# Chunk rows of a state-space scan taken in twos, on one Trainium2 core

## The chip, the cores and the metric

The kernel runs on one core of a Trainium2 chip. The metric is device time in microseconds (us) from the start to the end of one execution; the median of several runs is compared. Engines are named as in the profile: PE is the matrix engine (TensorE), PEld its weight load, DVE is VectorE, ACT is ScalarE, POOL is GpSimd, SP is the engine whose queue issues most of the DMAs.

## What is computed

One layer of a decoder with two branches: a causal pooling branch and a Mamba-2 (SSD) branch, over a prompt of 1024 positions and 8 short samples, merged by gates. The change touches only the prompt's SSD scan. In the reference it is this (cut to the loop body):

```python
def step(h, inp):                    # one chunk of Q = 128 positions
    xq, dq, Bq, Cq = inp
    acs = jnp.cumsum(dq * Ag, axis=1)
    ...
    decay = jnp.exp(jnp.where(mask, seg, -jnp.inf))
    cb = jnp.einsum('bign,bjgn->bijg', Cq, Bq)
    att = cb[..., None] * decay * dq[:, None]
    y = jnp.einsum('bijge,bjgep->bigep', att, xq)
    y = y + jnp.einsum('bign,bige,bgepn->bigep', Cq, jnp.exp(acs), h)
    last = acs[:, -1]
    w_in = jnp.exp(last[:, None] - acs) * dq
    h = h * jnp.exp(last)[..., None, None] + jnp.einsum('bjgn,bjge,bjgep->bgepn', Bq, w_in, xq)
    return h, y
```

There are 4 groups of 8 heads of 64 channels, a state of 128 and 8 chunks, so 32 steps, here called rows. Afterwards y + D*x is multiplied by silu(z), normalized, and multiplied by the rows of `w_ssm_out`.

## The kernel before

The work runs in three stages. First come the projections (up to some 765 us of the span). Then comes the chunk stage, some 765 to 1055 us, which the change concerns. Last comes a tail with the last output products.

**A row.** `chunk(g, c)` is a Python generator; each `next` on it traces one step of a row's instructions:

- load: DMAs on SP's queue for `dec` (the cumulated decays, broadcast to all partitions), `bc` (B and C) and `xb` (x)
- exponentials: `cE` by one ACT instruction (L1510), a triangular select on POOL (`far`, L1240), eight ACT exponentials of 128 columns (`exps`, L1244)
- middle: PE transposes x into the PSUM tile `px` (L1517), transposes B and multiplies B by C into `pbc` (L1519, L1520); ACT copies `bt` and C (L1522, L1524); DVE makes `xd` and `xw` (L1528, L1530) and multiplies `dec` and `cE` by PSUM columns (L1535, L1537)
- sums: PE's matmul `pu` of `bt` and `xw` with 512 columns (L1542, the state's increment), then `inner` (L1256, L1259): for each head one product of `xd` with `dec` and, from the second chunk on, one of the state with `cE`. Each has 64 weight columns, and two heads at a time write the upper and the lower half of the PSUM partitions. POOL and DVE make the new state `hn` (L1548, L1550), and DVE adds D*x into the sums (L1554)
- finish: DVE, ACT and POOL multiply by silu(z), split the result into two parts for the later product and sum its squares (`finish`, L1470 to L1481)

**Pieces.** Between these steps PE works on "pieces": `pieces()` yields after each block of 12 matmuls with 384 or 352 columns (`gemm_`, L221) into one of the three PSUM banks of `PA`. These are the products of the pooling branch and of earlier groups. `RATE = 2.56` pieces go with one row. DVE or ACT evacuates each.

**What sets the order.** In the chunk stage the instructions of PE and of SP's queue keep the order in which they are traced (`in_line(order)`, with `ORDER = ("PE","SP")`). Those of ACT, DVE and POOL are ordered by the planner, by its own estimate of times and with the traced order as priority; `tc.high_priority()` moves instructions forward in that priority. A tile's buffer is given to the next tile of the same tag when the last instruction that uses it, anywhere in the program, is done.

**The loop** (L1850 to L1871) takes one row at a time. In PE's order it gives: middle of row i+1, about one piece, `pu` and `inner` of row i, one or two pieces. PSUM: `PB` has four banks (`px`, `pbc`, and the sums `pi`), `PC` a single one (`pu`). From the ninth row on, one step of `wos` (the split of the output weights `w_o`, L1772 to L1825) goes with each row.

**The tail** starts with four more pieces and the sum of squares over partitions (L1903, L1904), from which ACT makes `rstd` (L1905, L1907). Later GpSimd adds rows of `x_prompt` in 16 accumulating DMAs (`plus_x`, L2065), the only DMAs that GpSimd issues.

## Time and profile before

| | us |
|---|---|
| runs | 1219.95, 1220.73, 1222.36; median 1220.73 |
| profiled execution, span from first to last instruction | 1219.3 |
| PE busy | 1203.2 (99% of the span) |
| DVE busy | 937.9 (77%) |
| POOL busy | 758.1 (62%) |
| ACT busy | 654.7 (54%) |
| chunk stage cut at 776.7 to 1053.5 | 276.8: PE 274.4, DVE 225.5, POOL 180.8, ACT 171.9 |

The profiled execution has no time of its own beside the span. The span is 1.4 us below the median of the runs, which is what lies around it; the granted clock is 0.998. In the rows of a timeline the columns are: start, length, engine, line, operation, tiles written and read, shapes, count of merged instructions, and in brackets the engine's idle time before it and what ended it. The lengths of matmuls overlap, since they are pipelined; the starts are what one subtracts. A PE instruction in float32 stands as two passes.

### The profile page before, as it was taken

To read this page: it belongs to the slowest core of one execution; us is meant where nothing else is said; L and a number is where in the kernel's file an instruction comes from. 1 tells how busy PE (TensorE), PEld (TensorE's weight loads), DVE (VectorE), ACT (ScalarE), POOL (GpSimd) and SP (SyncE) were. 2 spreads that over 40 slices of the span, in tenths; PEclk is the share of its full clock that TensorE was granted. 3 is DMA by queue.
4 is the path that set the end of the run, shared out by engine and by line. 5 is a ranking of instruction groups with operands and counts; after the bars stand their busy time and mean duration, and the time that the engine had idled before them with its cause. 6 is when DMAs were issued, how large, how long until landed. Compare 5 with 4: busy or idle time off the path is not lost.

```text
span 1219.3 us, 25493 instructions
## 1 busy us (share of the span) xinstructions
PE 1203.2 (99%) x9330; PEld 1127.1 (92%) x9330; DVE 937.9 (77%) x1587; ACT 654.7 (54%) x1491; POOL 758.1 (62%) x677
## 2 busy tenths in 40 slices
PE   9999999999999999999999999999999999999997
PEld 8879999999999999999989899989888898999885
DVE  6993788877989578876676664686877889679976
ACT  6854366565656656454544344566676656312435
POOL 1137868875978778664676766155677758422661
PEclk9999999999999999999999999999999999999999
DMA  9835455564565545443656566898779888585794
GB/s 347 307 136 212 134 155 179 157 232 151 165 188 181 171 149 187 137 143 122 205 187 210 172 198 215 317 314 265 264 257 293 270 279 279 186 313 174 233 213 150
DMA packets 169845, 257.48 MB, mean 211 GB/s; under 512 B 32048, under 2 KB 88120, under 8 KB 169720
## 3 DMA queue, kind: packets, MB, share of 16 engines
q1 hardware_dynamic: 89256, 163.38, 40.3%
q10 hardware_dynamic: 78160, 88.27, 21.4%
q0 software_dynamic: 2304, 4.20, 2.0%
q8 instruction: 74, 1.21, 0.4%
q14 instruction: 51, 0.42, 0.1%
HBM read 170.69 MB, written 85.10 MB: 210 GB/s over the span
## 4 chain that ended last, share of the span: by engine, by line
PE 84%; DVE 6%; DMA 5%; ACT 3%; issue 1%; POOL 1%; SPq 0%; ACTq 0%; DVEq 0%
PE mm L410 23%; PE ps L410 23%; PE mm L221 14%; PE pc L410 5%; PE ps L1256 2%; PE pc L1542 2%; PE ps L2042 2%; PE ps L2040 2%; PE ps L2041 2%; PE ps L1259 2%; DMA wo<-ph 1%; DMA Y<-in_x_prompt 1%; DMA v<-ys 1%; DMA dec<-acs_d 1%; PE ps L1517 1%
## 5 line engine op out<-in xcount | busy, mean ns | idle before, releaser
L148 POOL TENSOR_TENSOR wlo<-rawA,whi 128x512 fp32r<-128x512 f32 x120 | 173.7, 1452 | 81.4 <-ACT whi L145 77.4
L221 PE MATMUL mm<-Y,whi 128*128 128x352 f32 (+1 forms) x960 | 195.7, 334 | 0.8 <-DVE G L1975 0.6
L148 POOL TENSOR_TENSOR wlo<-raw,whi 128x512 fp32r<-128x512 f32 x90 | 149.1, 1665 | 61.4 <-ACT whi L145 51.3
L221 PEld LDWEIGHTS mm<-Y,whi 128*128 128x128 f32 x960 | 159.1, 188 | 7.6 <-issue 4.6
L1088 DVE SCALAR_TENSOR_TENSOR GA<-GA,cvT,GA 128x1112 f32<-128x1112 f32 x72 | 133.8, 1863 | 0.1
L410 PE MATMUL mm<-Y,whi 128*128 128x272 f32 x800 | 119.0, 291 | 0.1
L410 PE MATMUL ps<-Y,whi 128*128 128x272 f32 x800 | 117.4, 289 | 0.0
L145 ACT ACTIVATE whi<-rawA 128x512 fp32r<-128x512 f32 x120 | 75.1, 627 | 76.1 <-PE ps L410 37.7
L145 ACT ACTIVATE whi<-raw 128x512 fp32r<-128x512 f32 x90 | 56.0, 629 | 98.9 <-DVE raw L347 35.2
L410 PEld LDWEIGHTS mm<-Y,whi 128*128 128x128 f32 x800 | 106.8, 188 | 1.8 <-DVE h L1360 0.3
L410 PEld LDWEIGHTS ps<-Y,whi 128*128 128x128 f32 x800 | 106.9, 188 | 0.8 <-issue 0.7
L221 PE MATMUL mm<-Y,wlo 128*128 128x352 f32 (+1 forms) x480 | 98.5, 327 | 0.0
L1244 ACT ACTIVATE dec<-dec,acT 128x128 f32<-128x128 f32 x256 | 78.8, 389 | 29.2 <-POOL dec L1240 29.2
L221 PEld LDWEIGHTS mm<-Y,wlo 128*128 128x128 f32 x480 | 81.7, 188 | 0.0
L1474 POOL TENSOR_TENSOR Y<-xb,Y 128x512 fp32r<-128x512 f32 x32 | 41.2, 1287 | 54.4 <-ACT Y L1472 54.4
L285 POOL TENSOR_TENSOR pw<-pw,ph 128x512 fp32r<-128x512 f32 x40 | 65.8, 1644 | 14.1 <-ACT ph L283 8.2
L410 PE MATMUL mm<-G,whi 128*128 128x272 f32 x480 | 71.4, 290 | 0.0
L410 PE MATMUL ps<-G,whi 128*128 128x272 f32 x480 | 70.4, 289 | 0.0
L410 PE MATMUL ps<-Y,wlo 128*128 128x272 f32 x400 | 66.6, 288 | 0.0
L410 PE MATMUL mm<-Y,wlo 128*128 128x272 f32 x400 | 66.6, 288 | 0.0
L410 PEld LDWEIGHTS mm<-G,whi 128*128 128x128 f32 x480 | 64.0, 188 | 0.9 <-issue 0.4
L410 PEld LDWEIGHTS ps<-G,whi 128*128 128x128 f32 x480 | 64.2, 188 | 0.4 <-issue 0.3
(582 smaller groups left out, 3172.9 us busy)
## 6 DMA issues: line engine op xcount, KB each, us to landing
rawA<-in_w_in SPq DMA_DIRECT2D x62, 512.0 KB
dec<-acs_d SPq DMA_DIRECT2D x32, 512.0 KB
xbc<-GA ACTq DMA_DIRECT2D x24, 512.0 KB
Y<-wo SPq DMA_DIRECT2D x10, 1024.0 KB
pw<-in_w_ssm_out ACTq DMA_DIRECT2D x32, 256.0 KB
ws<-ph ACTq DMA_DIRECT2D x32, 256.0 KB
ws<-pw ACTq DMA_DIRECT2D x32, 256.0 KB
h<-in_state_ssm SPq DMA_DIRECT2D x32, 256.0 KB
```

Of the source, the lines that this page charges most:

```text
L145: ins = act(hi[:, :, :ncols], raw[:, :, :ncols], AF.Copy)
L148: (eng or nc.gpsimd).tensor_tensor(lo[:, :, :ncols], raw[:, :, :ncols], hi[:, :, :ncols].bitcast(F32), ALU.subtract)
L221: mm(ps[:, :n], w[k // 4][h][:, k % 4, :], r[k][:, o:o + n], start=(j == 0), stop=(j == len(terms) - 1))
L285: nc.gpsimd.tensor_tensor(raw.bitcast(F32R), raw, hi.bitcast(F32), ALU.subtract)
L410: mm(p, w[j // 8][:, k], A(k, s)[j // 4 == 1], start=(j == 0), stop=(j == 11))
L1088: V.scalar_tensor_tensor(d[:, :n], rp[:, k:k + n], cvT[:, 24 * k + mc:24 * k + mc + 1], d[:, :n], ALU.mult, ALU.add)
L1244: act(dec[:, h], dec[:, h], AF.Exp, bias=acT[:, c, 8 * g + h:8 * g + h + 1], scale=-1.0)
L1256: mm(o[hh], xd[:S, 2 * q + hh, :], dec[:S, 2 * q + hh], start=True, stop=state is None)
L1259: mm(o[hh], state[:, h * 64:h * 64 + 64], cE[:, h], start=False, stop=True)
L1474: nc.gpsimd.tensor_tensor(yl[g][:, :, o:o + S], v, yhc.bitcast(F32), ALU.subtract)
L1542: mm(pu, bt, xw.rearrange("p h d -> p (h d)"), start=True, stop=True)
L2040: mm(ps, hi, y[:, k, c0:c0 + cw], start=(first and k == 0), stop=False)
```

## The change

Rows are taken in pairs (a, b) with a even. A row's `pu` and state update become a step of their own ahead of `inner`. In PE's order a pair is now: middle of b, piece, `pu` of a, piece, middle of a+2, piece, `pu` of b, `inner` of a, `inner` of b, then the other two or three pieces. `inner` of a reads the state from before the pair (`before`). Tiles `dec`, `xb`, `cE`, `xd` and `xw` get one more buffer; the copies of B and C on ACT get priority; the first chunk's state is copied by DVE and not by ACT. The DMA scratch (SBUF kept for the descriptors of GpSimd's DMAs) is set to 1024 bytes a partition; unset, it is 16384.

```diff
@@ chunk
-        dec = ckt([P, 8, P], "dec", 3)
+        dec = ckt([P, 8, P], "dec", 4)
...
-        xb = ckt([P, 4, P], "xb", 5)
+        xb = ckt([P, 4, P], "xb", 6)
...
-            cE = ckt([P, 8, P], "cE")
+            cE = ckt([P, 8, P], "cE", 3)
...
-        act(bt, pbc[:, :P], AF.Copy)
-        if c > 0:
-            act(pbc[:, 2 * P:3 * P], Cf, AF.Copy)
+        with tc.high_priority():
+            act(bt, pbc[:, :P], AF.Copy)
+            if c > 0:
+                act(pbc[:, 2 * P:3 * P], Cf, AF.Copy)
...
-        xd = ckt([P, 8, 64], "xd", 2)
+        xd = ckt([P, 8, 64], "xd", 3)
...
-        xw = ckt([P, 8, 64], "xw", 1)
+        xw = ckt([P, 8, 64], "xw", 2)
...
         mm(pu, bt, xw.rearrange("p h d -> p (h d)"), start=True, stop=True)
-        pi = inner(xd, dec, P, *((hst[g], cE) if c > 0 else ()))
+        before = hst[g]
         hn = ckt([P, 512], "hst", 2)
         if c == 0:
-            act(hn, pu, AF.Copy)
+            V.tensor_copy(hn, pu)
...
         hst[g] = hn
-
+        yield
+        pi = inner(xd, dec, P, *((before, cE) if c > 0 else ()))
@@ the loop
+    next(seq[3])
+    for a in range(0, len(seq), 2):
+        b, due_ = a + 1, RATE * a
+        next(seq[b])
+        load_sz(b)
+        upto(due_ + 1)
+        next(seq[a])
+        ahead_(a + 2)
+        upto(due_ + 2)
+        ahead_(a + 2)
+        upto(due_ + 3)
+        next(seq[b])
+        next(seq[a])
+        next(seq[b])
+        ahead_(a + 4)
+        if a % NC == 0:
+            ends = sample_end(a // NC)
             next(ends)
-        if i % NC == 4:
+        if a % NC == 4:
             next(ends, None)
+        next(seq[a], None)
+        ahead_(b + 2)
+        ahead_(b + 4)
+        ahead_(a + 2, True)
+        upto(due_ + 4)
+        next(seq[b], None)
+        if a > 7:
             next(wos, None)
+            next(wos, None)
+        upto(RATE * (a + 2))
+        for j in (a, b):
+            next(seq[j], None)
@@ kernel
-    nc = _bacc.Bacc("TRN2", target_bir_lowering=False, num_devices=1)
+    nc = _bacc.Bacc("TRN2", target_bir_lowering=False, num_devices=1, dynamic_dma_scratch_size=1024)
```

`upto(n)` makes pieces until n have been made; `ahead_(n)` is the next step of row n if there is such a row, and with `True` the load of its silu(z).

More of the change, by code (lines that the diff above doesn't have):

```diff
@@ L1709, in tile_pool_ssd_step @@
     ck = right.__enter__()
-    for shape, tag, bufs in (((P, P), "bt", 2), ((P, 8, 64), "xd", 2), ((P, 8, 64), "xw", 1), ((P, 512), "ph", 3),
+    for shape, tag, bufs in (((P, P), "bt", 2), ((P, 8, 64), "xd", 3), ((P, 8, 64), "xw", 2), ((P, 512), "ph", 3),
                              ((P, 4, NS), "szs", 1), ((P, 512), "t2", 1), ((P, 512), "hst", 2)):
@@ L1849, in tile_pool_ssd_step, with upto, ahead_ @@
     order = tuple(mybir.EngineType[e] for e in ORDER)
-    for i in range(len(seq)):
-        if i + 1 < len(seq):
-            next(seq[i + 1])
-        products(i + 0.4)
-        if i > 0:
-            next(seq[i - 1], None)
-        next(seq[i], None)
-        if i % NC == 1:
-            ends = sample_end(i // NC)
-            next(ends)
-        if i + 3 < len(seq):
-            next(seq[i + 3])
-        if i + 1 < len(seq):
-            load_sz(i + 1)
-        if i + 2 < len(seq):
-            next(seq[i + 2])
-        next(seq[i], None)
-        if i % NC == 4:
-            next(ends, None)
-        if i > 7:
+    def upto(n):
+        nonlocal made
+        while made < n:
+            next(pc_, None)
+            made += 1
+    def ahead_(n, of=None):
+        if n < len(seq):
+            (load_sz if of else lambda j: next(seq[j]))(n)
+    next(seq[3])
[15 more added lines that the diff above has]
+            ends = sample_end(a // NC)
+            next(ends)
+        if a % NC == 4:
+            next(ends, None)
+        next(seq[a], None)
[5 more added lines that the diff above has]
+        if a > 7:
             next(wos, None)
-        products(i + 1.0)
+            next(wos, None)
+        upto(RATE * (a + 2))
+        for j in (a, b):
+            next(seq[j], None)
     next(seq[-1], None)
```

## The prediction

> **What bounds the kernel now.** I read the page first, then the time by engine cut to the chunk stage, the groups of instructions with shapes kept apart, the waits, and last PE's timeline of a few rows.

> ```profile
> span 1219.3 us, 25493 instructions
> PE 1203.2 (99%) x9330; PEld 1127.1 (92%) x9330; DVE 937.9 (77%) x1587; ACT 654.7 (54%) x1491; POOL 758.1 (62%) x677
> PE 84%; DVE 6%; DMA 5%; ACT 3%; issue 1%; POOL 1%; SPq 0%; ACTq 0%; DVEq 0%
> ```

> ```profile
> 776.70:1053.50 276.80, 274.43 (x2207) 243.40 (x2206) 225.54 (x382) 171.87 (x450) 180.79 (x209) 1.00 0.83 273
> ```

> PE holds 84% of the chain and idles 276.8 - 274.4 = 2.4 us of the chunk stage (last row: length, then PE, PEld, DVE, ACT, POOL, clock, DMA share). DVE idles 51 us there, ACT 105, POOL 96. So the stage is PE's, and a change to it is worth what it takes from, or puts into, PE's sequence. No matmul is removed. What is left are the joints between them, which a busy share of 99% hides. They show in one row of the scan:

> ```profile
> 889.46 0.60 PE L1517 MATMUL ps<-ident,xb 128*128 128x128 f32 x4
> 889.89 0.27 PE L1519 MATMUL ps<-ident,bc 128*128 128x128 f32 x1
> 890.00 0.39 PE L1520 MATMUL ps<-bc 128*128 128x128 f32 x2
> 890.14 0.88 PE L221 MATMUL mm<-Y,whi 128*128 128x352 f32 x4
> ...
> 892.15 1.02 PE L1542 MATMUL pc<-xw,bt 128*128 128x512 f32 x2
> 893.10 0.44 PE L1256 MATMUL ps<-dec,xd 128*64 128x128 f32 x4
> 893.37 0.39 PE L1259 MATMUL ps<-cE,hst 128*64 128x128 f32 x4
> 893.59 0.39 PE L1256 MATMUL ps<-dec,xd 128*64 128x128 f32 x4
> ...
> 894.46 0.39 PE L1256 MATMUL ps<-dec,xd 128*64 128x128 f32 x4
> 894.68 0.39 PE L1259 MATMUL ps<-cE,hst 128*64 128x128 f32 x4
> 895.00 0.96 PE L221 MATMUL mm<-Y,whi 128*128 128x384 f32 x4
> ```

> Four full-width passes of 128 columns take 889.89 - 889.46 = 0.43 us, so a pass of 512 columns takes 0.43 too, and `pu`'s two 0.86. But from `pu` to the first pass of `inner` it is 893.10 - 892.15 = 0.95: 0.09 lost on the way in. Inside `inner` a group of four passes takes 0.22 (893.37 to 893.59, 894.46 to 894.68). The first group takes 0.27, the last, up to the next piece, 0.32: 0.05 and 0.10 lost. So each visit to the 64-column shape costs 0.09 + 0.05 + 0.10 = 0.24 us of PE in which nothing streams. Other joints cost next to nothing: the piece that follows L1520 has its twelve matmuls done by 892.15. The weight loads tell of the same joint: they cannot run ahead into it.

> ```profile
> L1256 PEld LDWEIGHTS ps<-dec,xd 128*64 128x64 f32 x512 | 30.3, 136 | 25.0 <-issue 15.9 <-PE mm L221 3.0 <-ACT bt L1522 3.0
> ```

> The 25.0 us of idle weight loading over 32 rows (0.78 each) isn't the price itself: most of it lies under `pu`'s 0.86 us of streaming. The price is the 0.24.

> [...]

> **The change part by part.**

> *Two visits become one.* Per pair one way in and one way out go: `inner` of b follows `inner` of a in the same shape. 16 pairs x 0.24 = 3.8 us off PE's path. At most it is that. At least it is 16 x (0.24 - 0.10) = 2.2 us, if the second `inner`, which waits for other tiles and starts another PSUM bank, pays for its start what the dearer measured joint, the way out, costs. I take 3.8, because within one `inner` new weights and new partitions start every 0.22 us without a loss. That the two `pu` are now apart, one of them between pieces, costs nothing by the joint after L1520.

> *Stalls of PE.* The stage has few:

> ```profile
> PE ps L1519 <- DVE cE L1537: 1.6, 1, 1.6
> PE ps L1256 <- DVE cE L1537: 0.7, 1, 0.7
> DVE dec L1535 <- ACT ps L1524: 13.2, 11, 4.6
> DVE xw L1530 <- PE pc L1542: 3.0, 7, 0.9
> ACT cE L1510 <- DMA dec<-acs_d: 10.6, 5, 4.2
> ```

> Both PE stalls, 2.3 us, end with the multiply of `cE`. The priority for the copy of C (L1524) attacks the 13.2 us that DVE waits ahead of that multiply, and the second `xw` the 3.0. Neither is PE time by itself. These 2.3 us may go; a planner's new order may bring others. I put the balance at zero, between -2.3 and +2.3.

> *The middle of a+2* moves ahead of the pair's sums, so row a's `dec` and `cE` are ready a whole pair early. Row b's time between middle and sums is a piece, `pu`, a piece, a middle, a piece, `pu` and an `inner`. By the rows above a piece is 892.15 - 890.14 = 2.0, a middle 890.14 - 889.46 = 0.7 and an `inner` 895.00 - 893.10 = 1.9, so this is 3 x 2.0 + 2 x 0.9 + 2 x 0.7 + 1.9 = 11.1 us. The work of DVE in it is `xd`, `xw`, `dec` and `cE` of b, `xd` and `xw` of a+2, one `hn` and three evacuations, some 9 us by the groups' means (0.68 for the small ones, 1.2 for `dec` and `cE`, 0.5 an evacuation). It fits, with 2 us to spare; without that spare PE waits.

> *First-chunk copies.* Four leave ACT and go to DVE; nearest rows:

> ```profile
> L1546 ACT ACTIVATE hst<-pc 128x512 f32<-128x512 f32 x4 | 2.3, 586 | 0.3 <-PE ps L1256 0.3
> L1550 DVE TENSOR_TENSOR hst<-hst,pc 128x512 f32<-128x512 f32 x28 | 18.9, 676 | 0.4 <-PE pc L1542 0.4
> ```

> That is 4 x 0.68 = 2.7 us at most more on DVE, 2.3 less on ACT. DVE's 51 us of idle time cover it; uncovered it would be the 2.7.

> *Loads.* SP's queue keeps its traced order. The load of `dec` for a+4 waits for `inner` of a, and behind it stand B, C and x of that row, the samples' loads and the next weights. Weights are asked for two units, six pieces or 12 us, ahead, and the wait ends in PE's own order, so it costs nothing; if DMAs come later than now, the wait to look at is the 10.6 us of L1510 above (4.2 at worst), which lies on ACT. `dec` of a+4 has a pair's time before it is used. As for *buffers*, they add no instruction; their 14 KB a partition come out of the 15 KB that the scratch gives up.

> *The new state of b* gets the buffer of the state that `inner` of a reads, so POOL's multiply (L1548) now waits for that `inner`, with the other POOL work queued behind it. The state is needed only by the next pair, some 10 us on: no cost while POOL idles a third of the stage.

> *Sum.* 1220.7 - 3.8 = 1216.9 us as the median of runs; for the profiled span 1219.3 - 3.8 = 1215.5.

> **The rivals.**

> *The single `pu` bank (slower).* `pu` of b needs the bank that DVE frees by adding `hn` of a (L1550). Today a whole row, 8.6 us (276.8 / 32), lies between two `pu`; now it is piece, middle, piece: 4.7 us. DVE can be late:

> ```profile
> 954.71 1.02 PE L1542 MATMUL pc<-xw,bt 128*128 128x512 f32 x2
> 955.66 0.44 PE L1256 MATMUL ps<-dec,xd 128*64 128x128 f32 x4
> ...
> 956.56 0.87 DVE L1799 TENSOR_TENSOR R<-R,R 128x512 f32<-128x512 f32 x1 [2.51 <-DMA whi<-ws]
> ...
> 960.05 0.68 DVE L1800 TENSOR_TENSOR R<-R 128x512 f32<-128x512 f32 x1
> 960.65 0.68 DVE L1806 TENSOR_TENSOR t<-R,R 128x512 f32<-128x512 f32 x1
> ...
> 961.86 0.67 DVE L1550 TENSOR_TENSOR hst<-hst,pc 128x512 f32<-128x512 f32 x1
> ```

> Here the add ends at 962.5, 7.0 us after `pu` at 955.6; in the new order PE would wait 2.3 us. Against it: nothing hurried that add, and work on `w_o` (L1799 to L1806) went ahead of it. The point from which it decides is 3.8 / 16 = 0.24 us a pair. If a third of the pairs go as here, 5 x 2.3 = 11.5 us come back: 1228.4. I give all slower cases of this mechanism 0.14.

> *The gain doesn't arrive (no change).* Either the second `inner` pays its way in anew, or the tail doesn't start earlier:

> ```profile
> 1075.00:1100.00 25.00, 25.00 (x153) 24.87 (x152) 20.13 (x25) 2.56 (x5) 6.68 (x4) 1.00 0.95 349
> ...
> 1125.00:1150.00 25.00, 25.00 (x119) 21.13 (x118) 24.54 (x35) 10.01 (x24) 14.19 (x11) 1.00 0.84 260
> ```

> ```profile
> 1071.43 1.29 DVE L1961 TENSOR_TENSOR R<-rstd,R 128x1088 f32<-128x1088 f32 x1 [2.81 <-ACT rstd L1907]
> ```

> DMA is 95% busy at 1075 to 1100, and DVE 24.5 of 25 us at 1125 to 1150. If those loads, not PE, set the start of DVE's long stretch, the 3.8 us are waited out there: 1220.7. Against it: that stretch begins behind `rstd` (the row of DVE's timeline), whose matmuls stand in PE's order, and PE itself is full in both windows. With a balance of stalls that eats more than 1.4 us: 0.21.

> *The small scratch (slower).* GpSimd's 16 accumulating DMAs:

> ```profile
> q0 software_dynamic: 2304, 4.20, 2.0%
> ```

> ```profile
> L2065 POOL DMA_DIRECT2D R<-in_x_prompt x6: 869/1106/1740, 1121.1 to 1176.7; - x6
> DMA to landing us min/median/max: 3.8/6.9/11.0
> ```

> They have 2304 / 16 = 144 packets each. If a full ring made an issue wait for the landing of an earlier one, up to 11.0 us would hold POOL, in a stretch where DVE waits for nobody: 1216.9 + 11.0 = 1227.9. Against it: 16 issues over 60 us with 7 us to landing leave about two in flight. I give it 0.03.

> [...]

> *More than forecast.* Both stalls go and none comes: 1216.9 - 2.3 = 1214.6. It lies at the end of the forecast's own range.

> **How the numbers follow.** About 0.2%, 2.4 us, is what a measurement of this kernel can tell from no change. The forecast, with balances of stalls from -2.3 to +1.4, has 0.62 and its own range 1214.5 to 1218.3: all faster. No change has 0.21 (1218.3 to 1223.1). Slower has 0.14 + 0.03 = 0.17. The range for eight in ten reaches from a little under the forecast's own end to the end of "no change": 1213.5 to 1223.5.

> **What would show it.** In PE's timeline: sixteen stretches in which `inner` of two rows follow each other every 0.22 us per group, one step of 0.27 at the start and one of 0.32 at the end; weight loading idle before L1256's successor halved from 25 us. The chunk stage should be 3.8 us shorter, the tail as long as before. It would be wrong if PE waits for L1550 before `pu`, if the second `inner` starts with a step over 0.3 us, or if the idle time of PE in the stage rises above 2.4 + 1.4 us.

## The result, and the profile after

The changed kernel takes 1227.49 us (median of 6 runs, 1225.00 to 1230.93), the kernel before 1222.01 on the same chip (6 runs, 1219.95 to 1224.63): a ratio of 1.0050, interval [1.0035, 1.0065]. It is slower by 5.5 us where 1216.9 was forecast. The profiled execution took 1228.09 us. Its page, sections 1 and 4:

```profile
span 1226.4 us, 25488 instructions
...
PE 1201.7 (98%) x9330; PEld 1129.7 (92%) x9330; DVE 939.0 (77%) x1591; ACT 651.2 (53%) x1487; POOL 757.0 (62%) x677
...
PE 75%; DMA 8%; DVE 6%; issue 4%; POOL 3%; ACT 3%; SPq 0%; ACTq 0%; DVEq 0%; POOLq 0%
```

PE is busy 1.5 us less than before, but it holds 75% of the chain where it held 84%, and DMA has 8% where it had 5%. PE now waits. The time by engine shows where, cut to the chunk stage: from the middle of the first row to the first matmul of the sum of squares (columns: length, then PE, PEld, DVE, ACT, POOL, clock, DMA share). First before, then after:

```profile
766.41:1063.22 296.81, 294.19 (x2331) 262.80 (x2329) 238.55 (x403) 182.70 (x471) 185.26 (x214) 1.00 0.82 273
```

```profile
767.10:1068.82 301.72, 293.24 (x2330) 266.95 (x2329) 235.36 (x407) 179.22 (x467) 183.81 (x214) 0.99 0.80 268
```

The stage is 4.9 us longer. PE idles in it 301.72 - 293.24 = 8.5 us where it idled 2.6. The stage begins 0.7 us later, and from the last product to the end it takes 9.8 us where it took 8.3; between stage and last product both take 147.8. 0.7 + 4.9 + 1.5 is the 7.1 us between the two spans.

What was wanted did come. PE's timeline of the last pair, after:

```profile
1053.24 0.44 PE L1256 MATMUL ps<-dec,xd 128*64 128x128 f32 x4
...
1054.82 0.39 PE L1259 MATMUL ps<-cE,hst 128*64 128x128 f32 x4
1055.03 0.39 PE L1256 MATMUL ps<-dec,xd 128*64 128x128 f32 x4
...
1056.88 0.96 PE L221 MATMUL mm<-Y,whi 128*128 128x384 f32 x4
```

`inner` of b begins at 1055.03, 0.21 after the last group of a: no joint between the two. In rows that wait for nothing, two rows took 9.65 + 7.72 = 17.37 us of PE before, and a pair takes 17.03 (from one `inner` to the next, 821.64 to 838.67).

And this is the pair of rows 16 and 17, from the timeline of all engines:

```profile
922.71 2.15 ACT L1244 ACTIVATE dec<-dec,acT 128x128 f32<-128x128 f32 x7
...
922.91 1.50 DVE L1801 TENSOR_TENSOR R<-R,R 128x512 f32<-128x512 f32 x1 [2.35 <-DMA wo<-R]
...
925.42 0.27 ACT L1525 ACTIVATE ps<-bc 128x128 f32<-128x128 f32 x1
...
927.27 1.22 DVE L1812 TENSOR_TENSOR R<-t,R 128x512 f32<-128x512 f32 x1
...
928.41 1.21 DVE L1536 TENSOR_TENSOR dec<-dec,ps 128x1024 f32<-128x1024 f32 x1
...
929.76 0.70 PE L1256 MATMUL ps<-dec,xd 128*64 128x128 f32 x4 [3.00 <-DVE dec L1536]
...
930.80 0.70 PE L1259 MATMUL ps<-cE,hst 128*64 128x128 f32 x4 [0.34 <-DVE cE L1538]
...
931.28 0.64 PE L1256 MATMUL ps<-dec,xd 128*64 128x128 f32 x4
```

Row 17's copy of C (L1525) stands on ACT behind eight exponentials and ends at 925.7; on DVE four instructions of the split of `w_o` (L1801 to L1812) and two of the next row stand ahead of the multiply of `dec`, which starts at 928.4. PE waits 3.0 us. Then a group takes 0.43 (931.28 to 931.71) and not 0.22: the granted clock has gone to half (0.52 over 929 to 930, 0.50 from 930 to 935). This pair is 6.4 us longer than an undisturbed one: 3.3 us of that is the two waits, and nearly all of the rest goes with the half clock.

The waits of the stage after, cut, and then one of SP's queue:

```profile
DVE dec L1536 <- ACT ps L1525: 26.5, 13, 4.0
...
ACT cE L1510 <- DMA dec<-acs_d: 17.0, 5, 5.0
...
PE ps L1256 <- DVE dec L1536: 3.4, 2, 3.0
...
PE mm L221 <- ACT G L1745: 1.2, 2, 1.1
PE ps L1259 <- DVE cE L1538: 1.0, 2, 0.7
PE pc L1543 <- ACT bt L1523: 1.0, 1, 1.0
...
PE pc L1543 <- DVE hst L1551: 0.8, 1, 0.8
```

```profile
...
SPq L1496 <- POOL sq_acc L1481: 34.3, 9, 7.1
```

DVE's wait for ACT's copy has doubled (13.2 before), ACT's wait for `dec` has grown from 10.6 to 17.0. And on SP's queue something stands high that stood at 8.8 before: L1496, the load of silu(z), waits 34.3 us until POOL's `finish` (L1481) frees one of its three buffers. Behind it on the same queue stand the weights and the loads of `dec`, B, C and x.

### The profile page after: what moved, and what is told of

Read it like the earlier page. It is cut to its first block, busy times and chain, and to the rows that moved or that the text cites. A ratio compares the mean times of both kernels' runs of the same rounds, so it can differ in the third digit from the quotient of the medians.

```text
span 1226.4 us, 25488 instructions
## 1 busy us (share of the span) xinstructions
PE 1201.7 (98%) x9330; PEld 1129.7 (92%) x9330; DVE 939.0 (77%) x1591; ACT 651.2 (53%) x1487; POOL 757.0 (62%) x677
## 3 DMA queue, kind: packets, MB, share of 16 engines
q0 software_dynamic: 2304, 4.20, 2.1%
## 4 chain that ended last, share of the span: by engine, by line
PE 75%; DMA 8%; DVE 6%; issue 4%; POOL 3%; ACT 3%; SPq 0%; ACTq 0%; DVEq 0%; POOLq 0%
PE mm L410 23%; PE ps L410 23%; PE mm L221 13%; PE pc L410 5%; PE ps L1256 2%; PE ps L1259 1%; PE pc L1543 1%; DMA dec<-acs_d 1%; DMA Y<-in_w_ada 1%; DMA bc<-xbc 1%; PE ps L956 1%; DMA Y<-in_w_gate 1%; DVE tf L642 1%; PE pc L1344 1%; DVE dec L1536 1%
## 5 line engine op out<-in xcount | busy, mean ns | idle before, releaser
L221 PE MATMUL mm<-Y,whi 128*128 128x352 f32 (+1 forms) x960 | 201.3, 339 | 2.0 <-ACT G L1745 1.2
L221 PEld LDWEIGHTS mm<-Y,whi 128*128 128x128 f32 x960 | 161.0, 189 | 14.3 <-issue 10.1
L221 PE MATMUL mm<-Y,wlo 128*128 128x352 f32 (+1 forms) x480 | 98.7, 327 | 0.0
L221 PEld LDWEIGHTS mm<-Y,wlo 128*128 128x128 f32 x480 | 82.0, 188 | 0.0
L1240 POOL TENSOR_SCALAR_AFFINE_SELECT dec<-dec 128x1024 f32<-128x1024 f32 x32 | 34.9, 1093 | 46.1 <-ACT cE L1510 39.0
```

Of the source, the lines that this page charges most:

```text
L221: mm(ps[:, :n], w[k // 4][h][:, k % 4, :], r[k][:, o:o + n], start=(j == 0), stop=(j == len(terms) - 1))
L1240: nc.gpsimd.affine_select(dec, dec, [[0, 8], [1, P]], ALU.is_ge, FAR, base=0, channel_multiplier=-1)
```

## The experiments

All ratios are to the kernel before, on the same chip and in the same batch; "the changed kernel" is the one above. Theories at the start: L, the load of silu(z) at the head of a pair holds the later loads in SP's queue; W, two steps of the `w_o` split at once take DVE's spare time; P, POOL's multiply of the state waits for `inner` of a and holds POOL's other work; and, against all three, that the sums side by side are themselves the cost.

**sz_late: the load of silu(z) of b later.**

```diff
         next(seq[b])
-        load_sz(b)
         upto(due_ + 1)
@@
         ahead_(a + 4)
+        load_sz(b)
```

> The changed kernel (median 1227.5 us) with one call moved: the load of row b's silu(z) is traced behind the load of row a+4 instead of at the head of the pair. No other edit. Theory L (late loads): SP's queue stands at the head of the pair behind POOL's last instruction of an earlier row, which frees that buffer (34.3 + 12.2 us of such waits in the changed kernel, 9.7 before), so the broadcast decays come late, ACT stands (17.0 us) and row b's multiplies with it; L expects most of the 13 us of new PE stalls gone and 1215 to 1220 us. Theory P (POOL's state multiply of b waits for the sums of a) and theory W (two steps of the w_o split at once ahead of DVE's multiplies) expect no change, 1226 to 1229 us.

1217.47 us (1216.48 to 1219.83), 0.9973 [0.9962, 0.9984]: faster than both kernels. One moved DMA, with the orders that the planner then gave the other engines, is worth 0.77% of the time. The stage, and the waits in it:

```profile
766.99:1059.62 292.63, 289.17 (x2330) 264.60 (x2329) 233.64 (x407) 179.30 (x467) 183.67 (x214) 1.00 0.82 277
```

```profile
POOL hst L1549 <- PE ps L1259: 32.7, 9, 5.3
...
DVE dec L1536 <- ACT ps L1525: 20.5, 12, 3.2
...
ACT cE L1510 <- DMA dec<-acs_d: 16.3, 3, 6.1
...
PE ps L1256 <- DVE dec L1536: 1.8, 2, 1.1
```

PE idles 3.5 us and not 8.5, and its clock is full. SP's wait at L1496 for POOL falls to 13.7 us. POOL's wait for `inner` stays (32.7 us, 28.8 in the changed kernel): it costs nothing, so P falls. But ACT's wait for `dec` stays too, at 16.3, which L doesn't explain; the last two experiments come back to that.

**wo_spread: the two steps of the split apart.** One `next(wos, None)` goes behind the second `ahead_(a + 2)`.

> The changed kernel with one of the pair's two steps of the w_o split moved from the end of the pair to behind the middle of row a+2. Theory W: in the pair at 916 to 934 us four DVE instructions of that split (4.5 us) stand ahead of row b's multiply, and PE waits 3.0 us and then works at half clock; spread, these stalls (6.4 us) go: 1220 to 1223 us. Theory L and theory P: the multiply is late for another reason, 1226 to 1229 us.

1230.80 us, 1.0075 [1.0058, 1.0092]: slower still. W falls as the single cause: the stalls move to other places (3.9 us of PE before `pu` for `bt`, 2.9 for an evacuation by ACT).

**state_three: a third buffer for the state.**

```diff
-        xb = ckt([P, 4, P], "xb", 6)
+        xb = ckt([P, 4, P], "xb", 5)
...
-        hn = ckt([P, 512], "hst", 2)
+        hn = ckt([P, 512], "hst", 3)
```

> The changed kernel with a third buffer for the state, so that POOL's multiply for row b no longer waits for the sums of row a; x has five buffers and not six, to make the room. Theory P: POOL waits 28.8 us for those sums in the changed kernel, with the triangular select and the finish of rows behind it; without that wait most of the 13 us of PE stalls go: 1215 to 1220 us. Theory L: SP's wait for the buffer of silu(z) stays, no change, 1226 to 1229 us. Theory W: no change either.

1234.81 us, 1.0107 [1.0092, 1.0122]. The room for the third buffer came from `xb`, so two things changed. SP's load of x (L1506), which waited for neither in the changed kernel, now waits 56.4 us for ACT (L1473) and 31.1 for POOL (L1474), two steps of `finish`. It speaks against P, but not cleanly.

**sums_apart: `inner` of a right behind its `pu`, as before.** The `next(seq[a])` that makes `inner` of a moves up; the rest of the change stays.

> The changed kernel with the sums of row a back behind its own state increment, everything else as it is: 32 visits to the 64-column shape again. The price of a visit by the prediction is 0.24 us, by the two traces (17.38 us for two undisturbed rows before, 17.02 for an undisturbed pair) 0.33 to 0.35: 16 more cost 3.8 or 5.3 us, so 1231 to 1233 us if the stalls stay. By theory P the state multiply of b now finds its buffer free and the stalls fall too: 1220 to 1225 us. If the joint were worth nothing, and theory L holds, 1227 us.

1225.65 us, 1.0033 [1.0021, 1.0045]. Undisturbed rows take 9.65 and 7.72 again, yet the kernel is no slower than the changed one, where 1231 to 1233 us were expected if the stalls stayed. They didn't stay: PE idles 5.4 us in the stage and not 8.5. So the sums side by side aren't needed for a loss: the rest of the change is slower than before without them.

**late_apart: the late load and the sums apart.** Both edits.

> The kernel with the late load of row b's silu(z) (1217.5 us), and the sums of row a back behind its own state increment: 32 visits to the 64-column shape instead of 16, now without the stalls of SP's queue. The joint's price by the prediction: 0.24 us a visit, 1217.5 + 3.8 = 1221.3 us. By undisturbed rows and pairs of the traces 0.33 to 0.35: 1217.5 + 5.5 = 1223 us. If grouping the sums is worth nothing and the late load was all: 1217 to 1218 us. Some 2 us either way for stalls that the planner deals anew.

1222.25 us, 1.0003 [0.9994, 1.0013]. This is the kernel to hold against sz_late, since neither has a stall of weight:

```profile
765.81:1061.61 295.80, 294.17 (x2331) 262.76 (x2329) 241.46 (x407) 180.35 (x467) 185.32 (x214) 1.00 0.82 274
```

At a full clock PE is busy 294.17 us here and 289.17 with the sums side by side: 5.0 us, or 0.31 a pair. With the sums apart the rest of the change is worth nothing.

**late_xb5: the late load with five buffers for x.** `"xb", 6` becomes 5.

> The kernel with the late load of silu(z) (1217.5 us), with five buffers for x instead of six, the only other edit, as in the run with three state buffers (1234.8 us). Theory L (whatever makes SP's queue stand ahead of the loads of decays costs PE time): SP now stands at the load of x for POOL's finish (L1506, 31.1 us there) and the time goes up to 1224 to 1235 us. If that run was slow because of its third state buffer, 1217 to 1219 us here.

1227.43 us, 1.0052 [1.0035, 1.0068]. The load of x (L1506) now waits 63.3 us for ACT (L1473) and 16.1 for POOL (L1474), and the gain is gone. The sixth buffer is needed; with `xb` at 5 most of state_three's loss is there too. What of it is the wait and what is a new order on the engines, this run can't tell: DVE's order differs as well.

**late_noprio: the late load without the priority of the copies.** The `with tc.high_priority():` is left out.

> The kernel with the late load of silu(z) (1217.5 us), without the priority for ACT's copies of B and C. The prediction: the copies' order attacks DVE's wait ahead of row b's multiply. If the priority works, the time goes up, to 1220 to 1226 us, and DVE's wait for L1525 from 20.5 us to more; if the planner's order is the same without it, 1217 to 1218 us.

1219.41 us, 0.9987 [0.9978, 0.9996]. The priority seems to be worth 0.14%, but the two intervals overlap, and DVE's wait for the copy of C, which the priority was to shorten, is the same (20.4 us here, 20.5 in sz_late). So a gain by the priority isn't shown.

**scratch_alone: the kernel before with the 1 KB scratch.**

```diff
-    nc = _bacc.Bacc("TRN2", target_bir_lowering=False, num_devices=1)
+    nc = _bacc.Bacc("TRN2", target_bir_lowering=False, num_devices=1, dynamic_dma_scratch_size=1024)
```

> The kernel before with the DMA scratch set to 1024 bytes, no other edit. The prediction: no change, 1220 to 1222.5 us, and the 16 accumulating DMAs of GpSimd land after some 7 us as before. By the rival of the small scratch: up to 1233 us, with POOL held at L2065.

1228.81 us, 1.0066 [1.0046, 1.0087]: 7.5 us for an edit that changes no instruction and no engine's order. Once issued, GpSimd's accumulating DMAs land as quickly as before: after 3.9 to 9.8 us (median 5.3), before 3.8 to 11.0 (6.9). Most of the loss is elsewhere, at the head of the stage (timeline of the same kernel):

```profile
773.87 0.28 ACT L1522 ACTIVATE bt<-ps 128x128 f32<-128x128 f32 x1 [3.87 <-DMA gs<-u]
...
776.63 0.69 DVE L1528 TENSOR_TENSOR xd<-ps,dtT 128x512 f32<-128x512 f32 x1 [6.40 <-DMA gs<-u]
...
778.44 1.01 PE L221 MATMUL mm<-Y,whi 128*128 128x384 f32 x2 [3.88 <-DVE R L1725]
```

The first row's `bt` and `xd` wait for a store of `u` to land, a tile that neither of them reads. Before, they ran at 770.08 and 769.36. One guess is the addresses: if 15 KB less of scratch moves the other tiles, `bt` and `xd` may now lie where `u` was.

**scratch_pad: the same, with a 15 KB tile that nothing uses above the scratch.** It is there to give all other tiles their addresses of before; only the scratch is small.

```diff
+    lo_pad = ctx.enter_context(tc.tile_pool(name="lo", bufs=1)).tile([P, 3840], F32, name="lo_pad")
```

> The kernel before with the scratch of 1 KB, and at the bottom of SBUF, just above the scratch, a tile of 15 KB a partition that nothing uses. So every other tile has the address that it has in the kernel before, and only the ring of descriptors is smaller. Theory A (addresses: the 7.5 us of the scratch alone come from new tiles that overlap other, later-freed tiles): 1220 to 1223, no wait of bt or xd for the store of u at the start of the stage. Theory R (the ring: fewer descriptors delay GpSimd's transfers or others): 1227 to 1231, with the waits as in the run of the scratch alone.

1222.96 us, 1.0013 [1.0004, 1.0022]. The two waits are gone:

```profile
769.37 0.68 DVE L1528 TENSOR_TENSOR xd<-ps,dtT 128x512 f32<-128x512 f32 x1
...
769.73 0.28 ACT L1522 ACTIVATE bt<-ps 128x128 f32<-128x128 f32 x1 [0.62 <-PE mm L221]
```

So the loss at the head of the stage goes with the addresses: the 15 KB put back take it away. But the small scratch isn't free. The time is 2.0 us above that of the kernel before, with an interval clear of 1, and the scratch with its pad is all that differs. The last product stands at 1210.87 (before 1210.98); this span is 1.7 us longer behind it, 10.1 us against 8.3. The cause shows in POOL's issues, first before, then here:

```profile
1170.51 1.45 POOL L2065 DMA_DIRECT2D half<-in_x_prompt  x1
...
1174.81 0.87 POOL L2065 DMA_DIRECT2D m<-in_x_prompt  x1
```

```profile
1172.53 0.86 POOL L2065 DMA_DIRECT2D half<-in_x_prompt  x1 [1.09 <-DVE pc L2099]
...
1180.02 0.89 POOL L2065 DMA_DIRECT2D m<-in_x_prompt  x1 [2.70 <-DVE ps L2136]
```

DVE works at the same times in both (its add into this `half`, L2100, starts at 1169.54 before and at 1169.44 here), so the engines named in the brackets aren't what POOL waits for. From the first to the last of the 16 issues it takes 59.3 us before and 63.9 to 65.4 in all thirteen kernels with 1 KB (65.1 here, 64.6 in the changed kernel). So with the small scratch POOL is held back by 5 to 6 us, ahead of the issues, where the time to landing can't show it; what in the scratch does it, no view shows. What comes of it at the end differs from kernel to kernel: POOL's late products (L2133) run beside a DVE instruction (the first of L2201) that then takes 3.26 us where it took 0.74. In the changed kernel the same instruction (there L2223) takes 2.40, from 1201.16, while the products (there L2155) go on to 1203.0, and the end is 1.5 us longer; in sz_late it takes 0.87, and the end is as long as before. So the 1.5 us of the changed kernel most likely come from its small scratch. That the overlap with POOL's products is what stretches the DVE instruction isn't tested.

**late_both: the pair's other silu(z) load later as well.** `ahead_(a + 2, True)` moves to the end of the pair.

> The kernel with the late silu(z) load, and the pair's other silu(z) load, that of row a+2, moved to the end of the pair as well, behind its last pieces. Theory L (a silu(z) load that waits for its buffer holds the loads behind it): SP's wait at L1496, 13.7 us in the kernel with one late load, falls below 8; if it still cost something, 1214 to 1217, that is 0.5 to 3 us off, the two rows with stalls of 1.8 and 2.3 us becoming cheaper. Rival (that wait holds nothing that is urgent, and the two stalls come from ACT's late copy of C): the time stays at 1217 to 1219, and the two stalls stay or move. Second rival: the load comes too late for the product with silu(z), and that product waits for DMA: over 1219.

1220.20 us, 0.9991 [0.9981, 1.0001]: not better. SP's wait at L1496 for POOL stays at 12.5 us, so the edit didn't bring the short wait that L's forecast needed, and new stalls come in.

**late_old_order and early_new_order: queue and orders apart.** Moving one load in SP's queue also changed what the planner did with ACT, DVE and POOL. These two kernels separate the one from the other. Each engine's instructions of the stage are chained in a given order, `PLANNED`, taken from the other kernel; apart from the moved load the traced code is the same in all four kernels of the table below, and so are the addresses and PE's order.

```diff
+    for e_, seq_ in PLANNED.items():
+        of_e = [i for i in nc.cur_bb.bb.instructions[line[0]:] if i.engine == mybir.EngineType[e_]]
+        for x, y in zip(seq_, seq_[1:]):
+            tc.add_manual_dep(of_e[y], of_e[x].name, mybir.DependencyInfo(
+                mybir.DependencyClass.NoSync, mybir.DependencyReason.DATA), reason="planned")
     in_line(order)
```

> The late load of silu(z) changed not only SP's queue: the planner also gave ACT, DVE and POOL another order here and there (row by row, 55, 54 and 42 lines of the listings of their orders differ from the changed kernel's, of some 1470, 1540 and 640). Here SP's queue is that of the kernel with the late load, and ACT, DVE and POOL are held to the order that they have in the changed kernel. Theory Q (the wait in SP's queue is itself the cost: the loads behind it come late): 1216.5 to 1219.5, as with the late load. Theory O (the planner's other orders are the cost: in the pair of rows 16 and 17 the copy of C stands on ACT behind the next row's exponentials, and DVE's multiply of dec behind the split of the output weights): 1226 to 1229, and PE's stall at row 17 stays. Both in part: 1220 to 1225.

> The other half: SP's queue of the changed kernel, silu(z) of b at the head of the pair, with ACT, DVE and POOL held to the order that they have in the kernel with the late load. Theory Q: 1225 to 1229, SP's wait at L1496 some 34 us, and the stall at row 17 or others like it. Theory O: 1216.5 to 1219.5, with SP's wait still some 34 us and no stall of 3 us. Both in part: 1220 to 1225.

| | silu(z) of b at the head of the pair | late |
|---|---|---|
| ACT, DVE, POOL as in the changed kernel | 1227.49, 1.0050 [1.0035, 1.0065] | 1226.35, 1.0036 [1.0023, 1.0050] |
| as planned with the late load | 1229.13, 1.0053 [1.0038, 1.0069] | 1217.47, 0.9973 [0.9962, 0.9984] |

Neither half brings the gain: both theories, the queue alone and the orders alone, fall. No run holds a kernel to its own planned order, so what the chaining itself costs isn't measured apart; but the pairs without a stall are equally long in all four kernels, within 0.1 us. Each kernel's stalls, as the length of a pair over an undisturbed one (us; from one `inner` of a to the next):

| rows | 0/1 | 12/13 | 14/15 | 16/17 | 22/23 | 24/25 | 28/29 | sum |
|---|---|---|---|---|---|---|---|---|
| early, old orders (changed kernel) | 1.0 | 2.6 | 0.4 | 6.4 | 2.8 | 0 | 0 | 13.2 |
| late, old orders | 0 | 1.1 | 1.4 | 4.2 | 4.2 | 0 | 0.2 | 11.1 |
| early, new orders | 1.3 | 3.2 | 0 | 1.2 | 5.9 | 1.7 | 1.5 | 14.8 |
| late, new orders (sz_late) | 0 | 1.8 | 0 | 0 | 2.3 | 0 | 0 | 4.1 |

At rows 16 and 17 the orders decide. With the late load and the old orders (late_old_order, timeline of all engines) the picture is that of the changed kernel:

```profile
920.58 2.15 ACT L1244 ACTIVATE dec<-dec,acT 128x128 f32<-128x128 f32 x7
...
923.29 0.27 ACT L1525 ACTIVATE ps<-bc 128x128 f32<-128x128 f32 x1
...
924.90 1.21 DVE L1536 TENSOR_TENSOR dec<-dec,ps 128x1024 f32<-128x1024 f32 x1
...
926.25 0.44 PE L1256 MATMUL ps<-dec,xd 128*64 128x128 f32 x4 [1.61 <-DVE dec L1536]
```

In sz_late the copy of C ends ahead of those exponentials and the multiply goes between two instructions of the split, so PE runs through:

```profile
920.65 0.27 ACT L1525 ACTIVATE ps<-bc 128x128 f32<-128x128 f32 x1
...
921.04 0.76 DVE L1801 TENSOR_TENSOR R<-R,R 128x512 f32<-128x512 f32 x1 [2.35 <-DMA R<-in_w_o]
...
921.29 2.45 ACT L1244 ACTIVATE dec<-dec,acT 128x128 f32<-128x128 f32 x8
...
921.73 1.21 DVE L1536 TENSOR_TENSOR dec<-dec,ps 128x1024 f32<-128x1024 f32 x1
```

In rows 22 to 25 of early_new_order the queue decides:

```profile
985.28 0.53 SPq L1496 DMA_DIRECT2D sz<-z  x1
...
987.05 0.37 SPq L1236 DMA_DIRECT2D dec<-acs_d  x1
...
993.39 1.06 ACT L1510 ACTIVATE cE<-dec 128x1024 f32<-128x1024 f32 x1 [12.49 <-DMA dec<-acs_d]
...
1000.29 1.13 PE L1543 MATMUL pc<-xw,bt 128*128 128x512 f32 x2 [2.56 <-ACT bt L1523]
```

The load of silu(z) leaves SP's queue at 985.3, after a wait of 12.4 us, 9.7 of them for POOL, the load of `dec` behind it at 987.1; the same load leaves at 977.4 in sz_late, whose rows run 2.9 us earlier, so it is 6.7 us late. ACT, in order, stands 12.5 us before `cE`, and `bt`, planned behind that, is late for PE. An order that puts `cE` there is right only if the load is early.

## Why the prediction was wrong, point by point

*Two visits become one.* The mechanism was right, and the second `inner` pays nothing for its start (0.21 at 1055.03). The term was under-sized: 0.24 a visit and 3.8 us were forecast, 0.31 and 5.0 us measured by PE's busy time (late_apart against sz_late), 0.34 by undisturbed pairs. What is missing lies on the way out, which the prediction followed only up to the first start of the next piece. The piece behind the row that the prediction shows goes on like this (before):

```profile
895.80 0.86 PE L221 MATMUL mm<-Y,wlo 128*128 128x384 f32 x4
896.49 0.86 PE L221 MATMUL mm<-Y,whi 128*128 128x384 f32 x4
897.18 0.60 PE L1517 MATMUL ps<-ident,xb 128*128 128x128 f32 x4
```

Its first four matmuls take 0.80 us (895.00 to 895.80), the next four and the last four 0.69 each: 0.11 more, and 0.24 + 0.11 = 0.35. In time the two kernels differ by 3.7 us (1.0003 against 0.9973 of the kernel before), mainly since PE waits 1.8 us more in sz_late's stage; that this is close to the forecast 3.8 is luck. The idle time of L1256's weight loads fell from 25.0 to 16.3 us (14.4 in sz_late), not to half.

*Loads: the step that failed.* "SP's queue keeps its traced order. The load of dec for a+4 waits for inner of a ... so it costs nothing." I listed what stands behind the load of `dec` and didn't list what stands in front of it: `load_sz(b)`, moved to the head of the pair, where its buffer is freed only by the `finish` of an earlier row on POOL. That weights are asked for two units ahead helps only while nothing else in the queue waits longer. The wait in the queue isn't the whole price: late_old_order has it down to 10.2 us and still takes 1.0036. It costs what it does together with the orders of the other engines, which is the next term.

*Stalls of PE: the other term that failed.* "I put the balance at zero, between -2.3 and +2.3." In the stage PE's idle time rose by 5.9 us (2.6 to 8.5), and PE's busy time stands 4.1 us above that of sz_late (293.24 against 289.17), some 2.9 of it from the 5.8 us in which PE works at half clock (929.0 to 935.9). With 5.0 us off for the joints this is the 4.9 us by which the stage grew: -5.0 + 5.9 + 4.1. "A planner's new order may bring others" named the half of the cause that the two-by-two table shows, and priced it at nothing. The measured balance is +10.0 us.

*Row b's window.* "It fits, with 2 us to spare; without that spare PE waits." The list of DVE's work left out the two steps of the `w_o` split that go with each pair from the ninth row on. At rows 16 and 17 four of its instructions, 1.50 + 0.83 + 0.94 + 1.22 = 4.5 us, stand in the window, and PE waits 3.0. The sum itself has two slips: the list names one middle and the sum counts two (as listed the window is 10.4 us), and the parts named for DVE come to 7.3 us by the means given, not 9. Neither would have shown the stall; the split would. Spare time of an engine helps only if its order lets the urgent instruction go first: sz_late does the same work and waits 0.

*First-chunk copies* and *the new state of b* were right: POOL's wait for `inner` is as long in the fast kernel, and PE never waits for the copies in the changed kernel (in late_apart it does once, 1.4 us, L1547).

*Buffers and scratch.* "They add no instruction" was right and not enough: in the kernel before, the size of the scratch alone costs 7.5 us, most of it with waits for a store of `u` that are gone when the 15 KB are put back (in the changed kernel it costs nothing there: its `bt` and `xd` start at the head of the stage without such a wait). The rival of the small scratch, 11 us, was right in that POOL is held back, and far too large: with 1 KB it is 5 to 6 us at its issues (59.3 us from first to last before, 65.1 in scratch_pad), and the 1.5 us at the end of the changed kernel most likely come of that. What spoke against it, "16 issues over 60 us with 7 us to landing leave about two in flight", is an average: nine of the 16 come within 12.2 us (1168.12 to 1180.35 before), which makes some five in flight, by an estimate from the median landing of 6.9. How many transfers 1 KB has room for, and whether an issue waited for a landing, no run shows.

*The single `pu` bank* was the rival on the slower side, at 11.5 us. It is there and small: PE waited once, 0.8 us, for the add (L1551). The slower result came by another way.

*The tail* is as long as before (147.8 us) from the stage to the last product, as forecast; behind that product it is the 1.5 us longer.

## What to carry to other kernels

When a load moves forward in an in-order DMA queue, ask when its own buffer comes free, and count every load behind it, not only those behind the load of interest; the wait column of the queue's engine shows it (L1496 for POOL, 8.8 us before and 34.3 after). Where a planner orders some engines by estimated times, moving one DMA can change those orders too, and a gain or loss may belong to the pair of both (1226.35 and 1229.13 us with one of the two, 1217.47 with both): hold the orders fixed before you name a cause. And a memory setting that adds no instruction can still cost time, here 7.5 us alone and 2.0 with the room given back, so give it a run of its own.

## What the runs showed of the hardware

```profile
978.00:980.00 2.00, 0.60 (x7) 0.42 (x9) 2.00 (x3) 0.38 (x2) 2.00 (x3) 1.00 0.80 290
980.00:982.00 2.00, 2.00 (x31) 1.83 (x30) 1.97 (x5) 0.00 (x0) 2.00 (x5) 1.00 0.79 260
```

```profile
978.00:980.00 2.00, 0.68 (x14) 0.44 (x9) 1.16 (x2) 1.01 (x5) 2.00 (x4) 1.00 0.90 343
980.00:982.00 2.00, 1.10 (x14) 0.92 (x16) 2.00 (x3) 0.00 (x0) 2.00 (x4) 0.94 0.75 236
982.00:984.00 2.00, 2.00 (x22) 1.83 (x18) 1.81 (x5) 0.65 (x1) 1.21 (x2) 0.50 0.74 242
```

Both kernels wait there twice, for the multiplies of `dec` and of `cE`, with four matmuls between. In sz_late the waits are 1.15 and 0.69 us, and the clock stays full; in late_both 1.53 and 0.69, and it runs at half for 3.4 us (981.8 to 985.2). The same cut followed 1.61 and 0.60 us in late_old_order (927.1 to 930.5), a single gap of 2.56 in early_new_order (1001.4 to 1004.8) and one of 3.0 and 0.34 in the changed kernel (929.0 to 935.9, so 2.3 us into the longer gap). The pair of rows 22 and 23 is 2.0 us longer in late_both than in sz_late, for 0.4 us more of waiting.

The half clock lasted 3.4 us in three of these cases and 6.9 us in the changed kernel; the cut came after 2.2 to 2.6 us of idle time in all four, and not after 1.84 us (1.15 and 0.69) in sz_late.
